# GpSimd's sums of two gate jobs behind the softmax factors: one layer of a hybrid recurrent and attention encoder on one Trainium2 core

## The chip, the cores and the metric

The kernel runs on 1 core of one Trainium2 chip. The metric is the time on the device in microseconds, the median of several runs. A single profiled execution gives the trace. The engines are named as in the profile: PE is TensorE (PEld its weight loads), DVE is VectorE, ACT is ScalarE, POOL is GpSimd and SP is SyncE, which here only issues transfers.

## What is computed

One layer of an encoder trunk over 512 tokens of width 1024, all in float32: a half-step feed-forward block, a mixer of a recurrent branch and a sliding-window attention branch, and a second half-step feed-forward block. The part that matters here is the mixer.

```python
u = rms_norm(h, mix_pre_g)
q, k, v, xr, xg = split(u @ w_in)
hr = rg_lru(causal_conv(xr, conv_w, conv_b), ...)
y_a = (hr * gelu(xg)) @ w_lru_out
y_b = swa_sink_attention(q, k, v, sinks, bias) @ w_attn_out   # 16 heads, 4 groups of keys
g = sigmoid(u @ w_gate + b_gate).reshape(b, s, 2, d)
merged = g[:, :, 0] * y_a + g[:, :, 1] * y_b
h = h + rms_norm(merged @ w_o, mix_post_g)
```

The gate's weight `w_gate` is 1024 x 2048, which the kernel cuts into 16 column blocks of 128, called wg 0 to 15.

## The kernel before

Products are made in two float32r parts: a weight block of 128 x 1024 is split into `whi` (a rounded copy, ScalarE, L213) and `wlo` (the rest, VectorE, L214; both in `split2`), and each product takes three matmuls, `whi` by x, `wlo` by x and `whi` by the rest of x. The queues run in the order in which the program issues to them; nothing reorders them later. What is to be issued between matmuls is put on a list by `later(n, fn, rank)` (L197): `fn` is issued at the n-th mark from now. A mark is a call of `point()` (L201), which comes after every 12 matmuls of width 512 (L227) and after most groups of a pair job (L496). Of several items that are due at a mark, the one with the lower rank is issued first. All tiles called "slot" share one pool of 42 slots, so a new tile waits for the last readers of the one that was in its slot.

The attention runs as 16 steps, each for one group of 4 heads and 128 tokens. A step's scores are matmuls (L1292, L1293). VectorE adds the bias and takes the maximum (L1298), negates it into `ng` (L1301), and ScalarE takes the exponentials (L1306, L1307). `factors` (L1309) makes the reciprocal `d` on VectorE (L1310, L1311) and multiplies the four tiles of P by it on GpSimd (L1313); it is due four marks behind the scores at rank 3. Then TensorE transposes P (L1329), a split makes `PH` and `PL`, and two or four matmuls make the step's output (L1345, L1346), which VectorE adds up (L1354 or ACT L1356, then L1360) and ScalarE (L1364) and GpSimd (`OL`, L1365) split.

The last four column blocks of the gate, wg 12 to 15, are done as two pair jobs (`GatePairs`, L710). A pair job multiplies a 2 x 2 block form of two weight blocks with seven products in place of eight: it needs sums of the weight's quarters. `prep(m, i)` (L513) makes the operands of job m in five parts:

- part 0: the four sums S12 and S34, on GpSimd, in this order: L543, L544 (S12), L538, L539 (S34)
- part 1: the split of the first raw block (for a11 and a12)
- part 2: the split of S12 (for s1 and s2)
- part 3: the split of S34 (for s3 and s4)
- part 4: the split of a22

The first job's parts are issued at the marks in `GP_AT`, the second job's part 0 at the mark `GP_1` (L1382 to L1384), all at rank 3. The rest of the second job's parts are issued by `GatePairs.run` while the first job's groups run on TensorE. A job's groups are a11 (bank bu), s1 (bank bx), the job before's a22, s2 (bu again), s4 (bx again), s3 (bu again); ScalarE copies bu and bx in between (`q1` L729, `q5` L731, `u` L745, `v` L754), and a group that adds to a bank waits for the copy.

```python
GP_AT = (26, 28, 30, 32, 33)
GP_1 = 36
```

Of the kernel before, what the change touches and what calls it, by code (L numbers as in the profile page):

```python
# [51 lines left out]
def hybrid_layer(ctx: ExitStack, tc: tile.TileContext, a: dict, out: bass.AP):  # L52
# [10 lines left out]
    def slot(shape, dt=F32, name="s"):  # L63
        uid[0] += 1
        return sb.tile(shape, dt, tag="slot", name=f"{name}_{uid[0]}")

    def bank(name="ps"):
        uid[0] += 1
        return pp.tile([P, 512], F32, tag="ps", name=f"{name}_{uid[0]}")
# [127 lines left out]
    def later(n, fn, rank=1):  # L197
        uid[0] += 1
        due.append((now[0] + n, rank, uid[0], fn))
# [285 lines left out]
    def mm_s(wa, x, ps, more=False, mark=True):  # L485

        wh, wl = wa
        for k in range(4):
            s = slice(k * P, (k + 1) * P)
            xh, xl = x(0, k), x(1, k)  # L490
            first = k == 0 and not more
            pe.matmul(ps, wh[:, s], xh, start=first, stop=False, skip_group_check=True)  # L492
            pe.matmul(ps, wl[:, s], xh, start=False, stop=False, skip_group_check=True)  # L493
            pe.matmul(ps, wh[:, s], xl, start=False, stop=k == 3, skip_group_check=True)  # L494
        if mark:
            point()  # L496
# [213 lines left out]
    class GatePairs(Pairs):  # L710


        def run(self, gz, bias, tail):
            X, end = self.X, len(self.jobs) - 1
            assert st["get"] == st["split"] == self.k0, (st, self.k0)
            st["get"] = st["split"] = self.k0 + 2 * len(self.jobs)
            last = lambda: None
            for n, (nm, f) in enumerate(self.jobs):
                W = self.w.pop(n)
                tmp = slot([P, 4, 256], name="ct")  # L720
                q1, q5, u, v = (tmp[:, i, :] for i in range(4))
                c = gz[f // 2] = slot([P, 2, SEQ], name="g")
                bu, bx, bc = (bank("c")[:, :256] for _ in range(3))

                def gate(ps, i, c0, c1, c=c, f=f):
                    act.activation(c[:, i, c0:c1], ps, AF.Tanh, scale=0.5, bias=bias(f + i))

                mm_s(W["a11"], X["b11"], bu)
                act.activation(q1, bu, AF.Copy)  # L729
                mm_s(W["s1"], X["t1"], bx, mark=False)  # L730
                act.activation(q5, bx, AF.Copy)  # L731
                self.prep(n + 1, 1)
                last()

                def c11():
                    mm_s(W["a12"], X["b21"], bc, mark=False)
                    del W["a11"], W["a12"]
                    dve.tensor_tensor(out=c[:, 0, :256], in0=bc, in1=q1, op=ALU.add)


                if n < end:
                    c11()
                mm_s(W["s2"], X["t2"], bu, True)
                del W["s1"], W["s2"]
                act.activation(u, bu, AF.Copy)  # L745
                self.prep(n + 1, 2)
                mm_s(W["s4"], X["b22"], bx, True)
                dve.tensor_tensor(out=c[:, 0, 256:], in0=bx, in1=u, op=ALU.add)
                self.prep(n + 1, 3)
                if n == end:  # L750
                    tail()
                mm_s(W["s3"], X["t3"], bu, True, mark=False)
                del W["s3"], W["s4"]
                act.activation(v, bu, AF.Copy)  # L754
                dve.tensor_tensor(out=c[:, 1, 256:], in0=v, in1=q5, op=ALU.add)
                if n == end:
                    c11()
                gate(c[:, 0, :], 0, 0, SEQ)
                if n < end:
                    self.prep(n + 1, 4)  # L760
                    self.prep(n + 2, 0)
                self.raws(n + 3)

                def last(W=W, bu=bu, c=c, gate=gate):
                    mm_s(W["a22"], X["t4"], bu, True)
                    gate(bu, 1, 0, 256)
                    gate(c[:, 1, 256:], 1, 256, SEQ)

            tail()
            last()  # L770
# [609 lines left out]
    X4 = {"b11": uview(0, 0), "b21": uview(1, 0), "b22": uview(1, 1)}  # L1380
    pairs_m = GatePairs(("wg",), WGP, 16, X4)
    for i, p in enumerate(GP_AT):  # L1382
        later(p, lambda i=i: pairs_m.prep(0, i), 3)
    later(GP_1, lambda: pairs_m.prep(1, 0), 3)  # L1384
    for n, p in enumerate(GRAW_AT):
        later(p, lambda n=n: dma_one(pairs_m.k0 + n), 3)
    for n, p in enumerate(TB_AT):
# [93 lines left out]
NSLOT = 42  # L1481

WGP = 12
GP_AT = (26, 28, 30, 32, 33)
GP_1 = 36
GRAW_AT = (22, 23, 30, 31)
TB_AT = (32, 33, 34, 35)

# [64 lines left out]
```

## Time and profile before

| | us |
|---|---|
| median of 3 runs | 1129.06 |
| lowest and highest | 1128.47, 1129.76 |
| the profiled execution | 1128.72 |
| its span in the trace | 1126.9 |

The span is the time between the first and the last instruction in the trace; the profiled execution's own time is 1.8 us longer. The granted TensorE clock was 0.999 of full speed over the span. The stretch in question lies between 620 and 690 us from the span's start: the last attention steps, the last single gate blocks and the two pair jobs. In a row of a timeline the first number is the start, the second the time taken, then engine, line, operation, the tiles written and read, shapes and the count; a bracket names the engine's idle time before it and what ended it. A line can be that of a helper: L213 and L214 stand for all splits by `split2`.

### The profile page before, as it was taken

The numbers are of one execution on the slowest core, as the hardware profiler recorded it, in microseconds if no ns is written. First come the engines' busy times: TensorE is split into PE (matmuls) and PEld (weight loads), VectorE is DVE, ScalarE is ACT, GpSimd is POOL, SyncE is SP. The second block draws the span as 40 slices with busy tenths as digits, with TensorE's granted clock in tenths as the row PEclk, the third lists the DMA queues.
The fourth block names the chain that finished last, engine by engine and source line by source line (L and its number), as shares of the span: only waits on it lengthen the run. The fifth ranks groups of instructions, "written<-read, shape, count | busy, mean of one in ns | idle before, by whom it ended". The sixth has DMA issues, their size and how long they took to land.

```text
span 1126.9 us, 18141 instructions
## 1 busy us (share of the span) xinstructions
PE 1117.2 (99%) x7054; PEld 1012.9 (90%) x7054; DVE 838.4 (74%) x1238; ACT 623.4 (55%) x1114; POOL 369.0 (33%) x286
## 2 busy tenths in 40 slices
PE   9999999999999999999999999999999999999997
PEld 7899999988889977899888888889999999998886
DVE  5889989886436998887778877767898777975313
ACT  7755555574325778666656664456555555564211
POOL 0044444200000523242655863000966566700000
PEclk9999999999999999999999999999999999999999
DMA  9226563265314653156223235521333332255101
GB/s 337 108 82 149 136 129 113 76 224 168 98 53 148 157 118 102 38 171 241 60 91 113 92 134 186 211 90 38 113 107 92 102 113 86 88 199 170 40 19 56
DMA packets 40310, 136.54 MB, mean 121 GB/s; under 512 B 4880, under 2 KB 6800, under 8 KB 40224
## 3 DMA queue, kind: packets, MB, share of 16 engines
q1 hardware_dynamic: 36432, 123.28, 32.9%
q0 software_dynamic: 3504, 11.58, 5.3%
q8 instruction: 55, 0.90, 0.3%
q10 hardware_dynamic: 288, 0.52, 0.2%
q14 instruction: 31, 0.25, 0.1%
HBM read 121.74 MB, written 11.53 MB: 118 GB/s over the span
## 4 chain that ended last, share of the span: by engine, by line
PE 94%; DVE 2%; ACT 1%; POOL 1%; DMA 1%; issue 1%; DVEq 0%; SPq 0%; POOLq 0%; ACTq 0%
PE c L492 13%; PE c L493 13%; PE c L494 13%; PE acc L243 8%; PE acc L242 8%; PE acc L241 8%; PE f L223 8%; PE f L224 8%; PE f L225 8%; ACT P L1306 1%; DVE P L1298 1%; PE pt L1329 1%; PE tr L333 1%; DVE wlo L179 1%; PE f L849 1%
## 5 line engine op out<-in xcount | busy, mean ns | idle before, releaser
L492 PE MATMUL c<-uT,whi 128*128 128x256 f32 x528 | 149.8, 284 | 0.0
L494 PE MATMUL c<-uT,whi 128*128 128x256 f32 x528 | 149.7, 284 | 0.0
L493 PE MATMUL c<-uT,wlo 128*128 128x256 f32 x528 | 149.7, 283 | 0.0
L493 PE MATMUL c<-Xh,wlo 128*128 128x256 f32 x504 | 143.0, 284 | 0.0
L492 PE MATMUL c<-Xh,whi 128*128 128x256 f32 x504 | 143.0, 284 | 0.0
L241 PE MATMUL acc<-whi,hT 128*128 128x512 f32 x352 | 137.3, 390 | 0.0
L242 PE MATMUL acc<-wlo,hT 128*128 128x512 f32 x352 | 137.1, 390 | 0.0
L243 PE MATMUL acc<-whi,hT 128*128 128x512 f32 x352 | 137.1, 390 | 0.0
L223 PE MATMUL f<-uT,whi 128*128 128x512 f32 (+1 forms) x376 | 134.4, 358 | 0.0
L224 PE MATMUL f<-uT,wlo 128*128 128x512 f32 (+1 forms) x376 | 133.0, 354 | 0.0
L225 PE MATMUL f<-uT,whi 128*128 128x512 f32 (+1 forms) x376 | 133.0, 354 | 0.0
L214 DVE TENSOR_TENSOR wlo<-S,whi 128x1024 fp32r<-128x1024 f32 x88 | 129.1, 1466 | 5.1 <-ACT whi L213 4.2
L494 PE MATMUL c<-Xl,whi 128*128 128x256 f32 x456 | 129.3, 284 | 0.0
L213 ACT ACTIVATE whi<-S 128x1024 fp32r<-128x1024 f32 x88 | 90.4, 1054 | 25.8 <-DVE S L539 22.0
L493 PEld LDWEIGHTS c<-uT,wlo 128*128 128x128 f32 x528 | 101.5, 192 | 0.1
L492 PEld LDWEIGHTS c<-uT,whi 128*128 128x128 f32 x528 | 101.5, 192 | 0.1
L494 PEld LDWEIGHTS c<-uT,whi 128*128 128x128 f32 x528 | 101.5, 192 | 0.0
L492 PEld LDWEIGHTS c<-Xh,whi 128*128 128x128 f32 x504 | 96.9, 192 | 0.3 <-issue 0.3
L493 PEld LDWEIGHTS c<-Xh,wlo 128*128 128x128 f32 x504 | 96.9, 192 | 0.1
L494 PEld LDWEIGHTS c<-Xl,whi 128*128 128x128 f32 x456 | 87.7, 192 | 0.0
L223 PEld LDWEIGHTS f<-uT,whi 128*128 128x128 f32 x376 | 71.2, 189 | 10.9 <-issue 1.6
L225 PEld LDWEIGHTS f<-uT,whi 128*128 128x128 f32 x376 | 71.2, 189 | 9.8
(380 smaller groups left out, 2890.3 us busy)
## 6 DMA issues: line engine op xcount, KB each, us to landing
raw_w2a<-in_w2a_dram SPq DMA_DIRECT2D x22, 512.0 KB, 4.1
raw_w1b<-in_w1b_dram SPq DMA_DIRECT2D x22, 512.0 KB, 4.2
raw_w3b<-in_w3b_dram SPq DMA_DIRECT2D x22, 512.0 KB, 4.2
raw_w2b<-in_w2b_dram SPq DMA_DIRECT2D x22, 512.0 KB, 4.2
raw_w3a<-in_w3a_dram SPq DMA_DIRECT2D x21, 512.0 KB, 4.4
raw_w1a<-in_w1a_dram SPq DMA_DIRECT2D x20, 512.0 KB, 4.3
raw_wg<-in_wg_dram SPq DMA_DIRECT2D x16, 512.0 KB, 3.9
raw_xr<-in_xr_dram SPq DMA_DIRECT2D x8, 512.0 KB, 4.0
```

Source lines behind the costliest of these rows:

```text
L179: dve.tensor_tensor(out=lo, in0=r, in1=f32(hi), op=ALU.subtract)
L213: act.activation(hi, src, AF.Copy)
L214: dve.tensor_tensor(out=lo, in0=src, in1=f32(hi), op=ALU.subtract)
L223: pe.matmul(ps[:, c0:c1], wh[:, s], h_, start=k == 0, stop=False)
L224: pe.matmul(ps[:, c0:c1], wl[:, s], h_, start=False, stop=False)
L225: pe.matmul(ps[:, c0:c1], wh[:, s], l_, start=False, stop=k == KT - 1)
L241: pe.matmul(acc[n], x[:, 0, c], wh[:, s], start=first, stop=False)
L242: pe.matmul(acc[n], x[:, 0, c], wl[:, s], start=False, stop=False)
L243: pe.matmul(acc[n], x[:, 1, c], wh[:, s], start=False, stop=last)
L492: pe.matmul(ps, wh[:, s], xh, start=first, stop=False, skip_group_check=True)
L493: pe.matmul(ps, wl[:, s], xh, start=False, stop=False, skip_group_check=True)
L494: pe.matmul(ps, wh[:, s], xl, start=False, stop=k == 3, skip_group_check=True)
```

## The change

Three things are changed, and no instruction is added or removed.

- The first job's part 0 is due at mark 27 in place of 26 and at rank 4, behind a step's factors where both are due at one mark.
- The second job's part 0 is due at mark 37 in place of 36, at rank 4 too.
- In `GatePairs.run` the next job's part 2 moves from ahead of the s4 group to behind it, and part 3 from there to behind the s3 group and the job's first gate (L758).

```diff
                 act.activation(u, bu, AF.Copy)
-                self.prep(n + 1, 2)
                 mm_s(W["s4"], X["b22"], bx, True)
                 dve.tensor_tensor(out=c[:, 0, 256:], in0=bx, in1=u, op=ALU.add)
-                self.prep(n + 1, 3)
+                self.prep(n + 1, 2)
                 if n == end:
                     tail()
...
                 gate(c[:, 0, :], 0, 0, SEQ)
                 if n < end:
+                    self.prep(n + 1, 3)
                     self.prep(n + 1, 4)
                     self.prep(n + 2, 0)
...
     for i, p in enumerate(GP_AT):
-        later(p, lambda i=i: pairs_m.prep(0, i), 3)
-    later(GP_1, lambda: pairs_m.prep(1, 0), 3)
+        later(p, lambda i=i: pairs_m.prep(0, i), 3 if i else 4)
+    later(GP_1, lambda: pairs_m.prep(1, 0), 4)
...
-GP_AT = (26, 28, 30, 32, 33)
-GP_1 = 36
+GP_AT = (27, 28, 30, 32, 33)
+GP_1 = 37
```

On GpSimd's queue the first job's four sums stand behind four factors and ahead of one `OL`, where they stood ahead of these factors. The second job's four sums stand behind the last step's four factors and the next `OL`, where they stood ahead of both. On ScalarE's queue the second job's S12 stands behind an `OH` (L1364), where it stood ahead of it, and its S34 behind `v` and the gate, where it stood ahead of them. On VectorE's queue S12's rest stands behind the sum of the s4 group (L748 before), and S34's rest behind that of L755. SyncE's queue and the order of TensorE's matmuls are the same.

## The prediction

> **What bounds the kernel now.** I read the page first, then the waits of TensorE in the stretch the change touches, then the timelines of TensorE and GpSimd there.
>
> ```profile
> span 1126.9 us, 18141 instructions
> PE 1117.2 (99%) x7054; PEld 1012.9 (90%) x7054; DVE 838.4 (74%) x1238; ACT 623.4 (55%) x1114; POOL 369.0 (33%) x286
> ```
>
> TensorE is busy for 1117.2 of 1126.9 us. GpSimd, whose work the change moves, is busy a third of the time. So the change is worth what GpSimd makes TensorE wait, and costs what it makes TensorE wait anew. The waits of TensorE between 540 and 740 us are one row (total, times, longest):
>
> ```profile
> PE pt L1329 <- POOL P L1313: 1.1, 2, 0.6
> ```
>
> Twice the transposes of the softmax (tile pt) wait for the factors that GpSimd multiplies into P (L1313). The idle time understates it, since the engine also restarts. TensorE's timeline gives the whole price (start, us, engine, line, operation; in brackets idle time and its releaser):
>
> ```profile
> 635.95 0.49 PE L1329 MATMUL pt<-ident,P 128*128 128x128 f32 x3
> 636.97 0.76 PE L1329 MATMUL pt<-ident,P 128*128 128x128 f32 x5 [0.53 <-POOL P L1313]
> 637.49 0.48 PE L223 MATMUL f<-uT,whi 128*128 128x512 f32 x1
> ...
> 651.71 1.04 PE L1329 MATMUL pt<-ident,P 128*128 128x128 f32 x8
> 652.50 0.48 PE L223 MATMUL f<-uT,whi 128*128 128x512 f32 x1
> ...
> 668.45 0.56 PE L1329 MATMUL pt<-ident,P 128*128 128x128 f32 x3
> 669.58 0.77 PE L1329 MATMUL pt<-ident,P 128*128 128x128 f32 x5 [0.57 <-POOL P L1313]
> 670.10 0.48 PE L1345 MATMUL o<-PH,V 128*128 128x512 f32 x1
> ```
>
> Eight transposes that do not wait take 652.50 - 651.71 = 0.79 us until the next matmul. The two that wait take 1.54 and 1.65 us. The stalls are therefore 0.75 and 0.86 us, together 1.61 us, and this is all that the change can take away here.
>
> GpSimd's timeline shows why (S are the sums of L543, L544, L538, L539):
>
> ```profile
> 626.10 1.28 POOL L543 TENSOR_TENSOR S<-raw_wg 128x512 f32<-128x512 f32 x1
> ...
> 630.07 2.27 POOL L539 TENSOR_TENSOR S<-raw_wg,raw_wg 128x512 f32<-128x512 f32 x1
> 632.33 4.59 POOL L1313 TENSOR_SCALAR P<-P,d 128x256 f32<-128x256 f32 x4
> ...
> 638.78 4.14 POOL L1313 TENSOR_SCALAR P<-P,d 128x128 f32<-128x128 f32 x4 [1.18 <-DVE d L1311]
> ...
> 646.47 4.15 POOL L1313 TENSOR_SCALAR P<-P,d 128x256 f32<-128x256 f32 x4 [2.84 <-DVE d L1311]
> ...
> 655.29 3.63 POOL L1313 TENSOR_SCALAR P<-P,d 128x256 f32<-128x256 f32 x4 [3.97 <-DVE d L1311]
> 658.88 0.74 POOL L1365 TENSOR_TENSOR OL<-o,OH 128x256 fp32r<-128x256 f32 x1
> 659.58 1.27 POOL L543 TENSOR_TENSOR S<-raw_wg 128x512 f32<-128x512 f32 x1
> ...
> 663.55 1.31 POOL L539 TENSOR_TENSOR S<-raw_wg,raw_wg 128x512 f32<-128x512 f32 x1
> 664.82 4.70 POOL L1313 TENSOR_SCALAR P<-P,d 128x256 f32<-128x256 f32 x4
> ```
>
> Both times four sums stand ahead of four factors: 626.10 to 632.34 (6.24 us) and 659.58 to 664.86 (5.28 us). After the other two groups the idle time says that the factors waited for d, not for GpSimd.
>
> **Part 1: the first job's sums.** No instruction is added or taken away anywhere; only places in the queues change. The first job's four sums go behind the factors at 632.33, and ahead of one OL difference.
>
> ```profile
> 628.79 0.18 DVE L1311 RECIPROCAL d<-d 128x4 f32<-128x4 f32 x1
> ...
> 644.89 0.60 PE L1329 MATMUL pt<-ident,P 128*128 128x128 f32 x4
> ```
>
> The factors' d is ready at 628.97. Four factors of this size take 3.63 to 4.70 us by the rows above, so they end by 633.7 at the latest, over 2 us before the transposes at 635.95. That stall goes: 0.75 us. What is late next: the sums run from about 633.4 for 5.28 to 6.24 us, so to 638.7 or 639.6. OL (0.74) and the next factors (4.14) then end between 643.6 and 644.5. TensorE, 0.75 us earlier, takes these at 644.14, the fourth some 0.3 later. So between 0 and 0.1 us comes back; I take 0. The first job's splits are due three marks and more after the sums; its S12 is done some 2.6 us into them, and I cost this at nothing. The next groups (646.47 and 655.29) end at 650.62 and 658.92, and with TensorE 0.75 us earlier their covers shrink to about 0.3 and 0.1 us, so up to 0.2 us could be lost there; I take 0.
>
> **Part 2: the second job's sums.** These now stand behind the last factors (664.82) and one OL. Two VectorE operations of that last step were held up by the sums:
>
> ```profile
> 634.54 0.17 DVE L1301 TENSOR_SCALAR ng<-m 128x4 f32<-128x4 f32 x1
> ...
> 659.66 1.22 DVE L1301 TENSOR_SCALAR ng<-m 128x4 f32<-128x4 f32 x1
> ...
> 663.12 0.50 DVE L1310 TENSOR_TENSOR d<-d,es 128x4 f32<-128x4 f32 x1 [1.42 <-ACT es L1307]
> 663.65 0.18 DVE L1311 RECIPROCAL d<-d 128x4 f32<-128x4 f32 x1
> ```
>
> The negated maximum takes 0.17 us elsewhere and here 1.22, ending at 660.88, when the first sum ends (660.85). Without the sums beside it the exponentials can start 1.05 us earlier, and d is there at about 662.5 instead of 663.83. The factors then run from 662.5 and end between 662.5 + 3.63 = 666.1 and 662.5 + 4.70 = 667.2; TensorE wants them at 668.45 - 0.75 = 667.7. The second stall goes too: 0.86 us, and TensorE is 1.61 us ahead.
>
> **Part 3: the splits of the second job.** Now the sums come late for their readers: ScalarE rounds S12 and S34 (whi), VectorE takes the rest (wlo). In the old order:
>
> ```profile
> 665.49 1.08 ACT L213 ACTIVATE whi<-raw_wg 128x1024 fp32r<-128x1024 f32 x1
> ...
> 670.26 1.06 ACT L213 ACTIVATE whi<-S 128x1024 fp32r<-128x1024 f32 x1 [2.66 <-POOL OL L1365]
> ...
> 671.53 1.04 ACT L213 ACTIVATE whi<-S 128x1024 fp32r<-128x1024 f32 x1
> ...
> 673.64 0.62 ACT L213 ACTIVATE w<-raw_wg 128x512 fp32r<-128x512 f32 x1
> ...
> 675.88 0.38 ACT L729 ACTIVATE ct<-c 128x256 f32<-128x256 f32 x1
> ```
>
> ```profile
> 673.98 0.28 PE L492 MATMUL c<-Xb,whi 128*128 128x256 f32 x1
> ...
> 676.86 0.28 PE L492 MATMUL c<-Xb,whi 128*128 128x256 f32 x1
> ```
>
> The matmul at 673.98 is the second job's first with S12's split; the one at 676.86 adds to the bank that ScalarE copied at 675.88 (q1, L729), and may not start before that copy has ended (676.26). So ScalarE was only 0.6 us ahead of TensorE. In the changed queue ScalarE has, one behind the other: S12's whi, v (L754), the gate (L726), S34's whi, w, two PH, o, q1. Whatever S34's whi waits for, q1 waits for.
>
> With the factors' end in the middle, 666.7: OL to 667.4, S12 done after two of the four sums (half of 5.28) at 670.1, all four done at 672.7. S12's whi then ends at 671.15, and VectorE's wlo of 128x1024 asks for its operands while GpSimd is in its third sum. What that costs:
>
> ```profile
> 629.66 1.53 DVE L214 TENSOR_TENSOR wlo<-raw_wg,whi 128x1024 fp32r<-128x1024 f32 x1 [0.69 <-ACT whi L213]
> ...
> 647.53 1.39 DVE L214 TENSOR_TENSOR wlo<-S,whi 128x1024 fp32r<-128x1024 f32 x1 [0.17 <-ACT whi L213]
> ...
> 666.60 1.23 DVE L214 TENSOR_TENSOR wlo<-raw_wg,whi 128x1024 fp32r<-128x1024 f32 x1 [1.57 <-ACT whi L213]
> ```
>
> At 629.66 such a wlo stood beside the sums, and the sum at 630.07 took 2.27 instead of 1.31 us: 0.96 more. I take that, since it is the same pair: S34 is done at T = 673.7. ScalarE's whi (1.04) and the row from w's start to q1's end (673.64 to 676.26, 2.62) put q1's end at T + 3.66 = 677.35, and the matmul at 677.4. TensorE would have been there at 676.86 - 1.61 = 675.25: a new wait of 2.1 us, more than both that went. S12's wlo, at about 672.6, makes TensorE wait 0.1 us before that (it wants it at 673.98 - 1.61 + 0.12); the later wait swallows it, as it swallows any part of the 1.61 us that is not gained. So the change in the end is T + 3.7 - 676.86 = T - 673.15: **+0.5 us**.
>
> Bounds of T: with the factors ended at 666.1 and no pair of operations in each other's way, 666.1 + 0.74 + 5.28 = 672.1, so -1.0 us. With d not earlier (factors 663.85 + 4.70 = 668.55) and two wlo beside GpSimd, 668.55 + 0.74 + 5.28 + 2 x 0.96 = 676.5, so +3.3 us.
>
> [...] The wlo at 647.53 ran beside factors: it took 0.16 more than the one at 666.60, and its four factors 4.15 where the ones at 655.29 took 3.63. So the two shared the time with a loss of some 0.5 us, which the middle of the factors' end holds. [...]
>
> Behind this I cost nothing: SyncE issues the same transfers in the same order, and what follows the second job's matmuls moves with TensorE.
>
> **The rivals.** *The gain stays*: T comes by 672.6, because VectorE gets on faster without the sums in its way. For it: 0.17 against 1.22 us of ng. Against it: VectorE's wlo must meet the moved sums. It gives -0.5 to -1.6 us: 1127.5 to 1128.5. *The second job's sums become the bound* (slower): on GpSimd, from the last factors to S34, both wlo operations alternate with GpSimd's instructions and d comes no earlier; from T = 675.4 on the time is more than 2.26 us worse. For it: 2.27 and 4.70 in the rows; against: one of these alone is not enough. It gives +2.3 to +3.3: 1131.4 to 1132.4. *The change does not do what it says*: the first job's sums, now ahead of the factors at 638.78, push the stall to the next step and the rest comes out even: 1129.1. Against it: these end by 644.5 at the latest.
>
> **How the numbers follow.** The profiled execution took 1128.72 us (1.8 more than its span), 0.34 below the median of 1129.06. The sum gives 1128.72 + 0.5 = 1129.2 for it, and against the median 1129.6. Chances: forecast (T from 672.6 to 675.4, 1128.5 to 1131.3) 0.57; gain stays 0.20; slower rival 0.15; no effect 0.08. A measurement of this kernel tells about 0.2%, 2.26 us, from no change. No case reaches 2.26 us faster; for what I do not see I leave 0.03. Slower by more: 0.16. Within: 0.81. The range from 1127.8 to 1131.6 leaves out the ends of the two rivals.
>
> **What would show it.** Right: no bracket at either group of transposes; sums from about 633.4 and 667.4; ng of the last step near 0.2 us; S34's whi on ScalarE waiting for GpSimd; and TensorE idle for some 2 us before the second job's second matmul group on the same bank (L492), released by ct L729. Wrong: TensorE without idle time there (gain stays), or idle at the s1 group with more than 1 us on wlo, or a stall at the four transposes near 644 us. The whole would be wrong if TensorE gained idle time anywhere outside 630 to 690 us.

## The result and the profile after

| us | changed kernel | before, beside it |
|---|---|---|
| median | 1132.18 (1130.01 to 1132.89, 12 runs) | 1129.19 (1128.47 to 1130.08, 12 runs) |
| ratio to before | 1.0023, interval 1.0014 to 1.0032 | |
| profiled execution | 1132.35, span 1130.4 | 1128.72, span 1126.9 |

The change costs 3.0 us by the medians, and the predicted 1129.6 with its range to 1131.6 was too low. The changed kernel was timed again among the experiments (e5): 1131.1 beside 1129.68, ratio 1.0018 (1.0008 to 1.0027); this median lies inside the range. Of its 23 times ten lie between 1130.0 and 1131.1, ten between 1132.1 and 1133.0 and three between the two groups. Seven of the first 12 are in the upper group and three of the 11 of e5, so the median depends on how many of them fall there; what divides them is shown below.

The waits of TensorE between 540 and 740 us (us in total, times, longest), after:

```profile
PE c L492 <- ACT ct L729: 1.8, 1, 1.8
PE pt L1329 <- POOL P L1313: 0.5, 2, 0.3
```

Before, there was one row, the two stalls on P. Now there are two short ones on P, elsewhere, and a long wait for a copy by ScalarE. TensorE's timeline, after:

```profile
636.21 1.04 PE L1329 MATMUL pt<-ident,P 128*128 128x128 f32 x8
637.01 0.48 PE L223 MATMUL f<-uT,whi 128*128 128x512 f32 x1
...
644.62 0.41 PE L1329 MATMUL pt<-ident,P 128*128 128x128 f32 x2
645.28 0.33 PE L1329 MATMUL pt<-ident,P 128*128 128x128 f32 x1 [0.25 <-POOL P L1313]
645.86 0.33 PE L1329 MATMUL pt<-ident,P 128*128 128x128 f32 x1 [0.25 <-POOL P L1313]
...
669.19 1.04 PE L1329 MATMUL pt<-ident,P 128*128 128x128 f32 x8
...
676.68 0.28 PE L494 MATMUL c<-Xb,w 128*128 128x256 f32 x1
678.71 0.39 PE L492 MATMUL c<-Xb,whi 128*128 128x256 f32 x1 [1.75 <-ACT ct L729]
679.17 0.28 PE L492 MATMUL c<-Xb,whi 128*128 128x256 f32 x1
679.62 0.42 PE L492 MATMUL c<-Xb,whi 128*128 128x256 f32 x1
680.90 0.63 PE L1345 MATMUL o<-PH,V 128*128 128x512 f32 x1
```

Both groups of eight transposes that stalled run through without a bracket. But the four at 644.62 stall instead, and the matmul that stood at 676.86 before stands at 678.71. Behind it the matmuls slow down: a 128x256 that takes 0.28 at 679.17 takes 0.42 at 679.62, and a 128x512 takes 0.63 at 680.90. The windows view says why (stretch and its length, then busy time and count of PE, PEld, DVE, ACT and POOL, then the granted TensorE clock, the DMA share and GB/s):

```profile
670.00:679.00 9.00, 7.25 (x57) 6.85 (x55) 6.19 (x8) 6.28 (x11) 5.78 (x5) 1.00 0.40 130
679.00:683.00 4.00, 4.00 (x19) 3.62 (x19) 1.09 (x4) 2.48 (x5) 0.73 (x1) 0.57 0.53 139
683.00:690.00 7.00, 7.00 (x54) 6.75 (x54) 4.35 (x8) 2.66 (x6) 0.22 (x1) 1.00 1.00 394
```

From 679 to 683 us the granted clock was 0.57 on the mean. In the clock's records of the trace, that is half clock for 3.41 us, from 679.38 to 682.80; the records of the kernel before have no such stretch.

The same TensorE instructions, put side by side from both traces, give the account. At 10 us into the span the changed kernel is 0.26 us late, and it is 0.27 late still at 628.

| place (time before) | what happened | late by then, us |
|---|---|---|
| 637.6 | first stall gone, -0.75 | -0.48 |
| 646 | new stall at the four transposes, +1.19 | +0.71 |
| 668 | nothing more lost | +0.73 |
| 670.3 | second stall gone, -0.85 | -0.12 |
| 676.8 | wait for the copy q1 (ct, L729), +1.97 | +1.85 |
| 679.4 to 684 | half clock, +1.62 | +3.47 |
| 1119 | nothing more | +3.47 |

Why GpSimd and ScalarE were late for these two places, GpSimd's timeline after:

```profile
629.98 5.55 POOL L1313 TENSOR_SCALAR P<-P,d 128x256 f32<-128x256 f32 x4 [2.84 <-PE o L1346]
635.50 1.29 POOL L543 TENSOR_TENSOR S<-raw_wg 128x512 f32<-128x512 f32 x1
...
639.49 2.28 POOL L539 TENSOR_TENSOR S<-raw_wg,raw_wg 128x512 f32<-128x512 f32 x1
641.74 1.72 POOL L1365 TENSOR_TENSOR OL<-o,OH 128x256 fp32r<-128x256 f32 x1
643.44 2.37 POOL L1313 TENSOR_SCALAR P<-P,d 128x128 f32<-128x128 f32 x4
...
663.98 3.63 POOL L1313 TENSOR_SCALAR P<-P,d 128x256 f32<-128x256 f32 x4 [3.04 <-DVE d L1311]
667.57 1.26 POOL L1365 TENSOR_TENSOR OL<-o,OH 128x256 fp32r<-128x256 f32 x1
...
672.78 2.27 POOL L539 TENSOR_TENSOR S<-raw_wg,raw_wg 128x512 f32<-128x512 f32 x1
```

and ScalarE's:

```profile
675.09 1.06 ACT L213 ACTIVATE whi<-S 128x1024 fp32r<-128x1024 f32 x1 [1.47 <-POOL S L539]
676.05 0.61 ACT L213 ACTIVATE w<-raw_wg 128x512 fp32r<-128x512 f32 x1
...
678.27 0.38 ACT L729 ACTIVATE ct<-c 128x256 f32<-128x256 f32 x1
```

The first job's sums start at 635.50 and push the factors of the next step to 643.44, for transposes that want them at 644. The second job's S34 is done at 672.78 + 2.27 = 675.05; ScalarE stands at S34's whi until then and has w, two PH, o and q1 behind it, so q1 ends at 678.65, 3.60 us later.

### The profile page after: what moved, and what is told of

Its sections match the earlier page's. It is cut to its first block, busy times and chain, and to the rows that moved or that the text cites. A ratio compares the mean times of both kernels' runs of the same rounds, so it can differ in the third digit from the quotient of the medians.

```text
span 1130.4 us, 18139 instructions
## 1 busy us (share of the span) xinstructions
PE 1120.1 (99%) x7054; PEld 1015.1 (90%) x7054; DVE 837.7 (74%) x1238; ACT 623.8 (55%) x1114; POOL 369.0 (33%) x286
## 4 chain that ended last, share of the span: by engine, by line
PE 96%; POOL 1%; ACT 1%; DVE 1%; issue 0%; DVEq 0%; POOLq 0%
PE c L492 13%; PE c L493 13%; PE c L494 13%; PE f L223 9%; PE f L224 8%; PE f L225 8%; PE acc L243 8%; PE acc L242 8%; PE acc L241 8%; PE pt L1329 1%; PE tr L333 1%; PE s L1293 1%; PE s L1292 1%; PE f L847 1%; ACT P L1306 1%; PE f L848 1%
```

## The experiments

The theory: each stall on P that goes is bought with a wait of the job's own splits, the wait for q1 is set by when S34 is done, and the half clock follows from that wait. The rivals: the sums' new place alone costs (the stall near 645), or the splits' new places do.

**e1: the first job alone.** The second job's sums and all splits stay as before. The edit, in part:

```diff
-GP_AT = (26, 28, 30, 32, 33)
+GP_AT = (27, 28, 30, 32, 33)
-        later(p, lambda i=i: pairs_m.prep(0, i), 3)
+        later(p, lambda i=i: pairs_m.prep(0, i), 3 if i else 4)
```

> Only the first job's part 0 is moved (mark 27, rank 4); the second job's sums and splits stand as in the kernel before. Theory (nothing is gained at the first place): the stall of 0.75 us near 636 goes, but comes back one step later near 645 (0.6 to 1 us, on GpSimd's factors), and VectorE's and ScalarE's chain of the softmax is about 1.3 us late from there on; with the old order at the second place the last factors then end near 670.9, so the second stall grows from 0.86 to about 2 us. Time 1130.3 to 1131.2. Rival (the first move is good by itself, only the second costs): 0.75 us faster than before, 1128.4. If the grown stall also lowers TensorE's granted clock as the 1.75 us wait did in the changed kernel, 1.6 us come on top.

Measured: 1129.76 beside 1129.62, ratio 1.0002 (0.9993 to 1.001). TensorE gains 0.75 at the first stall, loses 0.71 near 645 and another 0.54 between 660 and 668, where the first job now waits for its own q1. The waits:

```profile
PE pt L1329 <- POOL P L1313: 0.8, 2, 0.6
PE c L492 <- ACT ct L729: 0.3, 1, 0.3
```

Neither expected time was met: the part is worth nothing that can be told, in either direction. The stall came back near 645, as the theory says, but the second one grew by 0.07 us and not to 2. What was taken at 637 is given back at 645 and by the job.

**e2: the second job alone.** The change with the first job's sums left at mark 26 and rank 3.

```diff
-GP_1 = 36
+GP_1 = 37
-    later(GP_1, lambda: pairs_m.prep(1, 0), 3)
+    later(GP_1, lambda: pairs_m.prep(1, 0), 4)
```

and the moved splits of the change.

> Only the second job's part 0 (mark 37, rank 4) and its splits are moved; the first job stands as before. Theory: the first stall of 0.75 us stays, the second of 0.86 goes; the chain of the softmax is not 1.3 us late, so S34 is done near 673.8 and q1 ends near 677.4: TensorE waits 1.4 us for ct L729 and the end is 0.5 us later than before without a change of the clock (1129.7), or 2.1 us later (1131.3) if a wait of that length lowers the granted clock. Rival (the whole loss comes from the first job's move): no wait for ct L729, 1128.3.

Measured: 1130.68 beside 1129.62, ratio 1.0008 (1.0000 to 1.0017), no run above 1131.24. In its profile the first stall is 0.72 us longer than before, since the softmax chain is late here too (see e9); the expectation had it stay as it was. TensorE gains 0.85 at the second stall and loses 1.40 at q1, with full clock throughout. S34 was done at 674.46, 0.59 before that of the changed kernel, and the wait is 0.5 shorter:

```profile
678.12 0.39 PE L492 MATMUL c<-Xb,whi 128*128 128x256 f32 x1 [1.24 <-ACT ct L729]
```

So the wait for q1 comes with the second job's part, and its length goes with the time of S34.

**e3 and e6: TensorE kept busy in the wait.** The change, with 16 (e3) or 8 (e6) matmuls of 128x256 ahead of the second job's s2, into a bank whose own group starts anew behind them, so that their result is not used. The edit of e3:

```diff
+                else:
+                    for _ in range(16):
+                        pe.matmul(bc, W["a12"][0][:, :P], X["b21"](0, 0), start=True, stop=True, skip_group_check=True)
```

> The changed kernel with 16 more matmuls of 128x256 ahead of the second job's s2 group, into the bank of its c11 group, which starts anew afterwards: their result isn't used. They need 1.9 us, about what TensorE waits there for ct L729. Theory (the wait costs 1.8 us by itself, and 1.6 more because TensorE idles and its granted clock halves for 3.4 us): no stretch at half clock near 680, about 1.6 us faster than the changed kernel, 1130.6. Rival (the slow matmuls behind the wait have another cause, such as memory contention with the late splits): the slow stretch stays, 1132.2.

> As with 16 matmuls, but 8: they fill 0.96 us, so TensorE is idle there for some 0.8 to 0.9 us only; the wait for ct L729 ends at the same time. Clock theory (an idle stretch of 1.2 us did not lower the clock, one of 1.8 us did): no half clock, the same time as with 16, 1131. Rival (any wait there lowers it): a stretch at half clock, about 1132.3, as the changed kernel.

Measured: e3 1131.08 (highest 1131.35), ratio 1.0012 (1.0003 to 1.0021); e6 1131.16 (highest 1131.87), ratio 1.0010 (1.0001 to 1.0019). With 16 the wait for q1 is gone from the list, with 8 it is 0.8 us. TensorE loses 2.0 us at this place in both profiles, as it does with the wait alone, and neither has half clock. So the added matmuls lie wholly inside the wait, as they must if ScalarE sets the end. Of the 22 executions of the two none reaches the changed kernel's upper group from 1132.1 on, with the same splits in the same late places. So the half clock came with the idle TensorE, and not with the late splits.

**e5: the changed kernel again.**

> The changed kernel once more, as the comparison for the next run on the same chip. Clock theory: a profile with the wait of about 1.8 us for ct L729 shows a stretch of 3.4 us at half clock behind it, and the median is about 1132, 2.5 to 3 us above before. Rival (the half clock was a freak of one execution): no such stretch, about 1130.5.

Measured: 1131.1 beside 1129.68, between the two expected times. The profiled execution took 1130.69, from the lower group. It waited for q1 as long as the first:

```profile
678.60 0.38 PE L492 MATMUL c<-Xb,whi 128*128 128x256 f32 x1 [1.74 <-ACT ct L729]
```

But its window shows a full clock:

```profile
680.00:690.00 10.00, 10.00 (x69) 9.27 (x68) 5.35 (x9) 6.57 (x13) 2.60 (x3) 1.00 0.89 332
```

The same stretch of the first profile of the changed kernel:

```profile
680.00:690.00 10.00, 10.00 (x65) 9.36 (x64) 4.50 (x8) 5.13 (x11) 0.95 (x2) 0.86 0.84 303
```

The two profiled executions differ by 1.66 us and TensorE's lateness at the end by 1.64 (3.47 and 1.83). The half clock is thus one execution's and not the other's, so the theory, which had it follow each such wait, was wrong for this profile. But it is no freak of one execution either. Its 1.62 us are about the distance between the two groups of times (1.9 between their medians), and the mean granted clock, noted for each execution, shows it too: 3.41 us at half clock take 0.0015 off the mean, and 11 of the 23 executions of the changed kernel have 0.997, eight of them in the upper group and one in the lower. None of the 99 executions of the nine variants and none of the 86 of the kernel before beside them is below 0.998.

**e4: the change with S34's split late.** The split of S34 moves from behind the gate into the second job, behind q5, so that q1 stands ahead of it on ScalarE.

```diff
                 act.activation(q5, bx, AF.Copy)
+                if n:
+                    self.w[n] = W
+                    self.prep(n, 3)
+                    self.w.pop(n)
...
                 if n < end:
-                    self.prep(n + 1, 3)
                     self.prep(n + 1, 4)
```

> The changed kernel, but S34's split (part 3) of the second job is issued behind that job's q1 and q5 copies, so on ScalarE q1 no longer stands behind it. Theory (q1 waits for S34's split in ScalarE's queue): q1 ends near 676, no wait for ct L729, no stretch at half clock; TensorE keeps what it has, 0.1 us ahead of the kernel before: 1129.0. Rival (S34 itself is too late for its readers): TensorE waits at the s4 group instead, on wlo of S34, by 1 us or more, 1130.1 to 1131.7.

Measured: 1129.3 beside 1129.62, ratio 0.9997 (0.9988 to 1.0006), near the theory's 1129.0. GpSimd ends S34 as late as in the changed kernel (672.93 + 2.27 = 675.20), and the wait for q1 is gone (line numbers in the kernels with the late split are 3 higher, in e10 5):

```profile
PE pt L1332 <- POOL P L1316: 0.5, 2, 0.3
PE c L493 <- DVE wlo L214: 0.3, 1, 0.3
```

What is left is the stall near 645 (+1.17) and 0.55 for S34's wlo at 679.9. So it was not the late sum in itself that cost the time, but that q1 stood behind its split.

**e7 and e8: the late split, with the first job's sums at mark 26 (e7) and 24 (e8).**

```diff
-GP_AT = (27, 28, 30, 32, 33)
+GP_AT = (26, 28, 30, 32, 33)
```

(24 in place of 26 in e8), at rank 3, on top of e4.

> Only the second job is changed, with S34's split behind q1 and q5. Theory (the first job's move gains nothing, S34's place is what costs): the first stall stays, no wait for ct L729, TensorE waits up to 0.5 us at the s4 group for wlo: 1129.2, the same as with the first job's move. Rival (the first job's move is worth its 0.75 us): 1130.0.

> As the run before, and the first job's part 0 at mark 24 at rank 3: two marks earlier than before instead of one later, into GpSimd's idle time of 5.8 us ahead of the factors at 620.87. Theory (the first stall goes only if the sums are out of the way of all factors): the sums end near 620.5 to 621.5, no wait of the transposes near 636 nor 645, about 1.2 us faster than before: 1128.2. Rival (the place of the first sums does not matter, since the softmax chain sets its own pace): 1129.2.

Measured, beside 1129.68: e7 1129.2, ratio 0.9994 (0.9985 to 1.0003), as its theory says; e8 1129.83, ratio 1.0002 (0.9993 to 1.0010), later than both of its expected times. In its profile e7 keeps the first stall, 0.75 us longer than before (the chain is late, as in e2), and is rid of the second. e8 is rid of both, but before them, at 623, TensorE waits 0.95 us for a VectorE operation. The waits of e8:

```profile
PE f L223 <- DVE o L1363: 0.9, 1, 0.9
PE c L493 <- DVE wlo L214: 0.3, 1, 0.3
```

Moving the whole block of four sums to the front of the stall, or behind it, moves the stall by one step.

**e9: the kernel before again.**

> The kernel before once more, for a second profile of it. In the profile shown, GpSimd's factors of the step ahead of the first job started at 620.87 us, in all the profiles since (changed kernel and variants) at 621.5 to 622.0. Theory: that lateness of 0.6 to 1.1 us is the execution's and not the change's, so here too the factors start at 621.5 or later, and the two waits of TensorE for the factors stay near 1.6 us together. Rival: the change or its variants bring it, and the factors start near 620.9 again.

Measured: 1129.04, a single execution. The factors of the step at 621 start at 621.17, with TensorE 0.39 us late from the start of the program, so relative to TensorE as early as in the first profile. The theory was wrong. The lateness begins at one wait of GpSimd; before, before again, and the changed kernel:

```profile
567.42 0.30 POOL L1275 MEMSET BT<- 64x256 f32 x1 [3.49 <-DMA BT<-bias_scr]
```

```profile
567.71 0.31 POOL L1275 MEMSET BT<- 64x256 f32 x1 [3.35 <-DMA BT<-bias_scr]
```

```profile
568.42 0.31 POOL L1275 MEMSET BT<- 64x256 f32 x1 [4.21 <-DMA BT<-bias_scr]
```

In the four profiles of kernels whose splits stand in their old places (before, before again, e1 and e11) GpSimd waits 3.35 to 3.54 us for this bias tile; in the nine others 4.09 to 4.66. The transfer of a weight block that runs beside it takes longer too, 4.8 to 5.8 us in the nine and 3.9 to 4.1 in the four, issued at the same point (us from issue to landing at the end of the row), before and after:

```profile
raw_lru<-in_lru_dram SPq DMA_DIRECT2D x1, 512.0 KB, 4.0
```

```profile
raw_lru<-in_lru_dram SPq DMA_DIRECT2D x1, 512.0 KB, 5.3
```

Counted from each program's start, the factors of the step at 610 are then 0.7 to 1.2 us later than before in the nine, and 0.3 at most later in the four. Up to the transfers the changed kernel issues the same instructions in the same order as before; why the transfers are slower was not found.

**e10: each job's sums in two parts.** S12 goes where all four sums stood before, S34 one mark later, behind the factors; S34's split of the second job is the late one of e4. The edit against the changed kernel, in part; `apart` is true for these two jobs, and `GP_AT` starts with 26 again:

```diff
+    later(GP_AT[0] + 1, lambda: pairs_m.prep(0, 5), 4)
+    later(GP_1 - 1, lambda: pairs_m.prep(1, 0), 3)
+    later(GP_1, lambda: pairs_m.prep(1, 5), 4)
...
-                if self.R is None:
+                if self.R is None and not self.apart:
                     sums34(e)
+            elif i == 5:
+                sums34(pool)
```

> Both jobs' sums in two parts: S12 where it stood before the change, S34 one mark later behind the softmax factors; splits of S34 of the second job inside the job, behind q5. Theory: the stalls for the factors shrink to about half (S12 is the shorter, 1.3 us of the 3.6), no wait for ct comes, and the time falls by 0.5 to 1.0 us: 1128.6 to 1129.2 beside 1129.7. Rival: each us taken from a stall ahead of a job comes back as a wait of the job for its own sums and splits, as in the two parts alone, and the time stays at 1129.4 to 1130.2.

Measured: 1127.49 (11 runs) beside 1129.83, ratio 0.9982 (0.9973 to 0.9991): better than expected, and ahead of both kernels. The list of TensorE's waits between 540 and 740 us is empty. The sum line of the windows from 620 to 690 us, of this kernel and of before:

```profile
sum 70.00, PE 69.98 PEld 62.57 DVE 54.20 ACT 45.13 POOL 46.66; mean PE 34.99 PEld 31.29 DVE 27.10 ACT 22.56 POOL 23.33
```

```profile
sum 70.00, PE 68.90 PEld 61.47 DVE 53.20 ACT 44.20 POOL 46.89; mean PE 34.45 PEld 30.73 DVE 26.60 ACT 22.10 POOL 23.45
```

GpSimd does as much as before, and TensorE has no idle time left. GpSimd's timeline of this kernel:

```profile
627.04 1.28 POOL L543 TENSOR_TENSOR S<-raw_wg 128x512 f32<-128x512 f32 x1
628.39 1.29 POOL L544 TENSOR_TENSOR S<-S,raw_wg 128x512 f32<-128x512 f32 x1
630.11 5.36 POOL L1318 TENSOR_SCALAR P<-P,d 128x256 f32<-128x256 f32 x4 [0.43 <-PE o L1351]
635.44 1.28 POOL L538 TENSOR_TENSOR S<-raw_wg,S 128x512 f32<-128x512 f32 x1
636.68 1.29 POOL L539 TENSOR_TENSOR S<-raw_wg,raw_wg 128x512 f32<-128x512 f32 x1
```

S12 fits into time in which GpSimd waited for d anyway (the bracket of 0.43 is what is left of it), and S34 takes 2.53 us behind the factors where the four took 6.27. The expectation had halved the stalls in proportion to the work; but a stall is only what exceeds the cover (0.75 of some 6 us of sums), so half the work takes all of it. TensorE is 1.17 us earlier at the end than in the profile before, counted from 10 us on; some 0.3 of what the two stalls gave is lost again at 665. The ratio's interval is 1.0 to 3.1 us, which holds the 1.6 us of the two stalls; the 2.3 us between the medians is more than they explain.

**e11: the change with the splits in their old places.** The edit against the changed kernel:

```diff
                 act.activation(u, bu, AF.Copy)
+                self.prep(n + 1, 2)
                 mm_s(W["s4"], X["b22"], bx, True)
                 dve.tensor_tensor(out=c[:, 0, 256:], in0=bx, in1=u, op=ALU.add)
-                self.prep(n + 1, 2)
+                self.prep(n + 1, 3)
...
                 if n < end:
-                    self.prep(n + 1, 3)
                     self.prep(n + 1, 4)
```

> The change with the second job's splits left where they stood before it. Theory (ScalarE's queue sets the end of q1): the split of S12 and of S34 stand ahead of the first job's gate on VectorE and ScalarE, so the activation that waits for S34 (done near 675) has v and the gate behind it, TensorE's wait ahead of 680 grows from 1.8 to 2.5 to 4 us, and the time is 1131.5 to 1133. Rival: moving the splits back is what costs, and with them in their old places the time is at most 1130.2.

Measured: 1131.87, ratio 1.0021 (1.0012 to 1.0030), within the theory's time. The wait is in two pieces, 2.3 us together, since v and the gate now stand behind S34's whi as well:

```profile
PE c L492 <- ACT ct L729: 1.4, 1, 1.4
PE c L492 <- ACT ct L754: 0.9, 1, 0.9
```

So the splits' new places are not what costs on TensorE. The whole program of this profiled execution stands 2.2 us later from its start (its full clock begins at 10.4 us, in the other profiles at 4.1 to 7.2); counted from there S34 is done at 674.4. By the prediction's formula, T - 673.15 with T for the end of S34, TensorE would be 1.2 late, and it is 2.1: with the same T the old places would cost 0.9 us more than the new ones. Their softmax chain is earlier, as e9 says, so the profiles lie closer together: behind q1 TensorE is 2.1 late here and 1.7 and 1.9 in the two profiles of the changed kernel, each counted from its start and without the half clock. The medians are alike (1131.87 beside 1132.18 and 1131.1) because about half of the changed kernel's executions have the half clock, and none of e11's shows it.

## Why the prediction was right or wrong

**What bounds the kernel: right.** With all waits of the stretch gone (e10) the time falls, by 1.0 us at the least by its interval.

**Part 1, the first stall: right; its cover: wrong.** The 0.75 us went to the hundredth. But of what comes back, 0 to 0.1 us was forecast and 1.19 came: the stall at the four transposes, which the prediction had named as a sign of being wrong. The four factors were bounded at 4.70 us; beside two wlo of VectorE they took 5.55. They also began 1.0 later (629.98 for 628.97): 0.26 of that is the later start of this execution, and the rest is the late softmax chain, which begins at the bias tile (e9). So the sums ran from 635.50 instead of 633.4. In these rows one wlo costs GpSimd 0.96 us: 2.27 against 1.31 for a sum, 2.28 again at 639.49, and (5.55 - 3.63) / 2. The prediction had this number and used it for the second job only. The stall itself made no difference in the end, as the prediction had said: the later wait swallowed it. That the two shrunk covers behind it cost nothing was right (+0.71 at 646, +0.73 at 668).

**Part 2: right in what it gains, wrong in when.** The second stall's 0.85 us went (0.86 forecast), and the factors took 3.63, the lower bound. The negated maximum took 0.17 us in place of 1.22:

```profile
660.99 0.17 DVE L1301 TENSOR_SCALAR ng<-m 128x4 f32<-128x4 f32 x1
```

But it began 1.33 later than before (660.99 for 659.66), since the whole chain was late, and so the factors began at 663.98 and not at 662.5. They ended at 667.6, behind both bounds (666.1 and 667.2). TensorE, 0.73 late by then, still came 1.6 us after that, so the gain was safe, but the lateness went into T.

**Part 3, the new wait: right in place, cause and formula; T was off by 1.35 us.** TensorE waited for q1 (1.97 us of lateness, 2.1 forecast), and q1 ended 3.60 us after S34 (3.66 forecast). The formula for the change, T - 673.15, gives +1.9 for T = 675.05, and TensorE was +1.85 late; for e5 (T = 674.94) +1.8 against +1.83; for e2 (T = 674.46) +1.3 against +1.36. The term that was mis-sized is T = 673.7. The four sums took 6.25 us as forecast; the OL ahead of them ended at 668.80 instead of 667.4, of which 0.87 is the factors' later end (667.57, the softmax chain late; 0.26 of it is again this execution's later start) and the rest OL itself, 1.26 us beside VectorE's wlo instead of 0.74. This wlo:

```profile
666.89 1.34 DVE L214 TENSOR_TENSOR wlo<-raw_wg,whi 128x1024 fp32r<-128x1024 f32 x1 [1.57 <-ACT whi L213]
```

The wlo did not wait for the fourth factor, which ran until 667.6: it started beside it and took 1.34 us, where the one at 666.60 before, beside factors too (four in 4.70), took 1.23. But the OL that met it took 0.52 us longer than the 0.74 of the one at 658.88 before, which the prediction had put into its sum.

**The cost of the wait beyond its length: the step that failed.** The sum counted a wait of 2 us as 2 us, and put what follows at nothing, with no row for it: "what follows the second job's matmuls moves with TensorE". In one of the two profiles, and by the times in about half of the 23 executions, the matmuls behind the wait ran at half clock for 3.41 us and lost another 1.62. This, with the 1.35 of T, is the distance between +0.5 and the 3.47 of the profile. By the medians the change costs 3.0 us the first time and 1.4 the second, as more or fewer executions have the half clock. The lower group's median is 1130.8, inside the range; which side of 1131.6 the median fell on was left to this share, which the prediction did not have.

What decides it is open. The clock's records of the first profile of the changed kernel show 672.43 us of full clock, 3.41 of half clock and 443.73 of full clock, which is 197, 1 and 130 times 3.413 us; in the twelve other profiles the one stretch of full clock lasts 327 or 328 times 3.413 us (1119.57 us, 328 times, in that of the kernel before). So in these records the clock switched on a grid of such steps. The step ahead of the half clock, from 675.97 to 679.38, holds the whole wait of 1.75 us. But in e5 the step from 675.18 to 678.59 holds 1.73 us of idle time, and no half clock follows. In e2 the grid cuts the wait of 1.24 into 0.83 and 0.40, and the two waits of e11 (0.94 and 1.43) lie in two steps. The length of the wait alone does not settle it: 1.75 us without matmuls was followed by half clock in one profile, 1.74 us (e5) and 1.24 us (e2) were not.

**The rivals.** The slower one had the price right (1131.4 to 1132.4) by luck, for another reason: it asked for T beyond 675.4, and T stayed at 675.05. That the gain stays did not come true in the change, but does in e10. Of the third, that the change does not do what it says, the mechanism came true in the first half: the first job's sums pushed the stall to the next step (+1.19; the factors ended at 645.8, not by 644.5), and alone this half comes out even (e1). The rest did not come out even.

## What to carry to other kernels

When work on a helper engine is moved later, price it by the queue of its reader: everything behind the instruction that now waits moves with it, and it may be cheaper to move that one instruction (e4) than the work. A stall is the excess over its cover, so look for a part of the moved block that is enough: two of four sums, put behind the factors, took both stalls away, while moving all four only moved the stalls. Where a change adds a wait of TensorE of 2 us or so, allow for the clock behind it: here, behind a wait of 1.75 us, it cost 1.62 us on top in one of two profiles, and by the times in about half of 23 executions.

## What the runs showed of the hardware that was not expected

- One wait of 1.75 us in a TensorE that is busy for 99% of the span was followed, 0.7 us after its end, by half clock for 3.41 us; in another execution of the same program, with a wait of 1.74, it was not. By the times and the mean clock it came in about half of 23 executions. Waits of 1.24 (e2), 0.95 (e8) and 0.8 us (e6), and two of 0.94 and 1.43 us some 3 us apart (e11), showed it in no profile. In all 13 profiles the clock's switches lie whole steps of 3.413 us apart: 327 or 328 steps in twelve, and 197, 1 and 130 in the first of the changed kernel.
- Two transfers near 563 us took longer in nine profiles than in four others (GpSimd's wait for one 4.09 to 4.66 us against 3.35 to 3.54), whose kernels differ only in work some 50 us and more behind them. The difference went with the splits' places, 100 us behind them. GpSimd's chain was later by up to 1.2 us, and this entered T. Its cause stays open.
